# Second feed-forward block: four rounds of sevens instead of three, sums laid out anew

## The chip, the core and the metric

The kernel runs on one core of one Trainium2 chip. It is one launch that computes a whole decoder layer. The metric is the device time of that launch in microseconds, from its first to its last instruction and what lies around it. Three runs of the kernel before gave 854.62, 854.68 and 855.35 us; the median is 854.68 us. TensorE is PE in the profile, VectorE is DVE, ScalarE is ACT, GpSimd is POOL and SyncE is SP.

## The reference

The layer works on 512 tokens of width 1024 in f32, with an inner width of 22 x 128 = 2816:

```python
def swiglu(x, w_gate, w_up, w_down):
    return (jax.nn.silu(x @ w_gate) * (x @ w_up)) @ w_down

x = x + 0.5 * swiglu(rms_norm(x, g_ffn1[l]), w_ffn1_gate[l], w_ffn1_up[l], w_ffn1_down[l])
...          # attention in a window, convolution, attention to 256 memory tokens, and their output matrix
x = x + 0.5 * swiglu(rms_norm(x, g_ffn2[l]), w_ffn2_gate[l], w_ffn2_up[l], w_ffn2_down[l])
```

The change concerns the two feed-forward lines, and the second above all.

## The kernel before

Activations lie transposed: a tile has 128 features on the partitions and the 512 tokens along the row. Every f32 operand is cut in two parts, a rounded one ("hi", made by an ACT cast) and what is left of it ("lo", made by a DVE subtraction). One product then is three matmuls, hi x hi, hi x lo and lo x hi, which all add to one PSUM bank.

**The walk over f.** A block goes through 22 slices f of the inner width. For each slice it needs gate and up (the function `fast`, from f = 3 in the second block), and `hidden` then cuts the result, the tile u of slice f, in hi and lo. Gate and up come as seven products of 256 tokens each in place of eight, in Strassen's manner. For this `make_sums` builds four sums of the two raw weight tiles g and u on DVE (two go to s12, two to s43). Each of the seven products has 4 k-tiles x 3 = 12 matmuls, so a slice has 84.

**The rounds.** The down projection isn't kept for the end. The 22 slices are grouped in rounds, and while the slices of one round are computed, the products of the round before are put in between: one step, a quarter of a round, for every slice. In a plain round a step is `down`: for two output tiles it runs slices x 2 halves x 3 matmuls each, and DVE adds the result to x (L749). In a round "by sevens" (`inside`) four slices make two pairs, and a step is seven products of 2 x 3 = 6 matmuls, 42 in all. It needs its own sums: `four` builds four of the weights (L147 to L150), and `paired` builds four of the hidden slices once for each pair (L498 to L501) and cuts them (L478). ACT halves the results into four staging tiles (cosb, sinb, mk, mv; L516), and four DMAs that POOL issues add them to x (L547). The DMA with mk goes to the same tile of x as the one with cosb and is issued when that has landed; the one with mv likewise after sinb.

**The last round.** When slice 21 is computed, the steps that are left over ("post") run, and then `seven` for g = 0 to 3: four times 42 matmuls, whose order on PE, DVE and ACT is the order of the code. The first, g = 0, adds a part of its result to x0 and x1 through two DMAs of POOL (L567). Each `leave` (L575) reads PSUM and x on DVE and sends a tile to the output; the leaves of g run in the round g + 1, behind the weight work that is done ahead there.

**The order.** Outside the last round a scheduler of the framework sets each engine's order by its priorities, bound by the marks in the code (`issue_after`). The buffers are rings. Four raw weight tiles (wraw) are filled by SP's queue. Four cut weight tiles (w) are written by ACT and DVE as soon as PE is through with the one used four items earlier. Three "sum" tiles hold the sums.

## Time and profile before

| | before |
|---|---|
| median of three runs | 854.68 us |
| the profiled execution, its own time | 856.12 us |
| its span, first to last instruction | 854.0 us |
| PE busy | 844.8 us (99%), 6325 matmuls |
| DVE busy | 734.6 us (86%), 1288 instructions |
| ACT busy | 503.7 us (59%), 894 instructions |
| POOL busy | 77.4 us (9%), 86 instructions |
| granted TensorE clock, mean over the span | 0.998 |
| first matmul of the down products after slice 21 | 822.04 us |
| first matmul of `seven`, g = 0 | 830.20 us |
| last matmul starts | 849.24 us |

Times of the trace count from the start of the span. A row of the timeline gives start, length, engine, line and operation, and how many instructions it stands for; in square brackets stands how long the engine was idle before it and what ended that. Two instructions of an engine overlap a little, so the distance between two starts, not the length, says what an instruction costs its queue.

### The profile page before, as it was taken

To read this page: it belongs to the slowest core of one execution; us is meant where nothing else is said; L and a number is where in the kernel's file an instruction comes from. 1 tells how busy PE (TensorE), PEld (TensorE's weight loads), DVE (VectorE), ACT (ScalarE), POOL (GpSimd) and SP (SyncE) were. 2 spreads that over 40 slices of the span, in tenths; PEclk is the share of its full clock that TensorE was granted. 3 is DMA by queue.
4 is the path that set the end of the run, shared out by engine and by line. 5 is a ranking of instruction groups with operands and counts; after the bars stand their busy time and mean duration, and the time that the engine had idled before them with its cause. 6 is when DMAs were issued, how large, how long until landed. Compare 5 with 4: busy or idle time off the path is not lost. (4 is left out here: it accounts for less than half of the span.)

```text
span 854.0 us, 16045 instructions
## 1 busy us (share of the span) xinstructions
PE 844.8 (99%) x6325; PEld 782.2 (92%) x6325; DVE 734.6 (86%) x1288; ACT 503.7 (59%) x894; POOL 77.4 (9%) x86
## 2 busy tenths in 40 slices
PE   8999999999999999999999999999999999999997
PEld 5889999999999999988676788889999999999997
DVE  7998899697877897959988986799879988987897
ACT  7455567655564444632848764666545577767454
POOL 0000002210000000400000021220000022212000
PEclk9999999999999999999999999999999999999999
DMA  7435338764454334232001332873423378787524
GB/s 274 125 88 147 93 120 198 173 161 137 124 160 125 124 111 131 76 99 62 13 26 38 88 100 86 197 160 105 126 93 111 112 182 189 158 199 169 142 74 124
DMA packets 43419, 107.19 MB, mean 126 GB/s; under 512 B 4176, under 2 KB 8784, under 8 KB 43344
## 3 DMA queue, kind: packets, MB, share of 16 engines
q1 hardware_dynamic: 32032, 85.99, 32.3%
q0 software_dynamic: 10160, 18.62, 12.9%
q10 hardware_dynamic: 1152, 1.57, 0.6%
q8 instruction: 49, 0.80, 0.4%
q14 instruction: 26, 0.21, 0.1%
HBM read 88.07 MB, written 2.10 MB: 106 GB/s over the span
## 5 line engine op out<-in xcount | busy, mean ns | idle before, releaser
L675 PE MATMUL mm<-bh,w 128*128 128x256 f32 x888 | 245.7, 277 | 0.3 <-ACT kept L693 0.2
L676 PE MATMUL mm<-bl,w 128*128 128x256 f32 x888 | 245.3, 276 | 0.0
L677 PE MATMUL mm<-bh,w 128*128 128x256 f32 x888 | 245.3, 276 | 0.0
L675 PEld LDWEIGHTS mm<-bh,w 128*128 128x128 f32 x888 | 166.7, 188 | 0.8 <-ACT kept L693 0.7
L676 PEld LDWEIGHTS mm<-bl,w 128*128 128x128 f32 x888 | 166.7, 188 | 0.1
L677 PEld LDWEIGHTS mm<-bh,w 128*128 128x128 f32 x888 | 166.7, 188 | 0.0
L214 ACT CAST w<-wraw 128x1024 fp32r<-128x1024 f32 (+2 forms) x107 | 106.7, 1001 | 81.8 <-PE mm L421 35.7
L219 DVE TENSOR_TENSOR w<-wraw,w 128x1024 fp32r<-128x1024 f32 (+2 forms) x101 | 117.8, 1171 | 12.5 <-ACT w L214 11.4
L219 DVE TENSOR_TENSOR w<-s,w 128x1024 fp32r<-128x1024 f32 x90 | 109.8, 1220 | 17.9 <-ACT w L214 14.4
L214 ACT CAST w<-s 128x1024 fp32r<-128x1024 f32 x90 | 94.5, 1051 | 41.3 <-PE mm L677 24.9
L420 PE MATMUL mm<-hl,w 128*128 128x256 f32 (+1 forms) x392 | 114.5, 293 | 0.1
L421 PE MATMUL mm<-hh,w 128*128 128x256 f32 (+1 forms) x392 | 114.2, 292 | 0.0
L419 PE MATMUL mm<-hh,w 128*128 128x256 f32 (+1 forms) x392 | 114.0, 293 | 0.1
L420 PEld LDWEIGHTS mm<-hl,w 128*128 128x128 f32 x392 | 73.6, 188 | 2.8 <-DVE hl L634 0.7
L419 PEld LDWEIGHTS mm<-hh,w 128*128 128x128 f32 x392 | 73.4, 188 | 2.9 <-ACT hh L633 0.8
L421 PEld LDWEIGHTS mm<-hh,w 128*128 128x128 f32 x392 | 73.6, 188 | 2.1
L419 PE MATMUL mm<-xh,w 128*128 128x512 f32 x176 | 69.8, 401 | 0.6 <-ACT w L230 0.5
L420 PE MATMUL mm<-xl,w 128*128 128x512 f32 x176 | 69.3, 394 | 0.5 <-DVE xl L431 0.5
L421 PE MATMUL mm<-xh,w 128*128 128x512 f32 x176 | 69.0, 392 | 0.0
L704 ACT ACTIVATE t<-t 128x512 f32<-128x512 f32 x37 | 23.4, 633 | 52.1 <-DVE t L703 52.0
L160 DVE TENSOR_TENSOR s<-wraw 128x512 f32<-128x512 f32 x37 | 25.5, 689 | 32.2 <-DMA wraw<-in_wgu 31.9
L513 PE MATMUL mm<-h,w 128*128 128x256 f32 x180 | 49.8, 277 | 0.4 <-DVE w L219 0.4
(299 smaller groups left out, 1857.6 us busy)
## 6 DMA issues: line engine op xcount, KB each, us to landing
wraw<-in_wgu SPq DMA_DIRECT2D x86, 512.0 KB, 3.8
wraw<-in_wd SPq DMA_DIRECT2D x38, 512.0 KB, 3.7
wraw<-in_win SPq DMA_DIRECT2D x12, 512.0 KB, 3.5
x<-cosb POOLq DMA_DIRECT2D x12, 256.0 KB, 5.5
x<-sinb POOLq DMA_DIRECT2D x12, 256.0 KB, 5.3
x<-mk POOLq DMA_DIRECT2D x12, 256.0 KB, 4.4
x<-mv POOLq DMA_DIRECT2D x12, 256.0 KB, 5.4
wraw<-in_wd SPq DMA_DIRECT2D x8, 384.0 KB, 3.5
```

The lines of the kernel that those rows point to most:

```text
L160: nc.vector.tensor_tensor(s12[:, l], u[:, l], u[:, r], op=ALU.add)
L214: nc.scalar.copy(hi[:, :cols], raw[:, :cols])
L219: nc.vector.tensor_tensor(lo[:, :cols], raw[:, :cols], hi[:, :cols].bitcast(F32), op=ALU.subtract)
L419: PE.matmul(ps[:, t], wh[:, w], hi(k)[:, t], start=one, stop=False, skip_group_check=cut > 1)
L420: PE.matmul(ps[:, t], wh[:, w], lo(k)[:, t], start=False, stop=False, skip_group_check=cut > 1)
L421: PE.matmul(ps[:, t], wl[:, w], hi(k)[:, t], start=False, stop=end, skip_group_check=cut > 1)
L513: PE.matmul(ps, w[1][:, s], hi, start=False, stop=q == 1, skip_group_check=not first)
L675: PE.matmul(ps, wh[:, c], bh[k][:, block], start=one, stop=False, skip_group_check=not first)
L676: PE.matmul(ps, wh[:, c], bl[k][:, block], start=False, stop=False, skip_group_check=not first)
L677: PE.matmul(ps, wl[:, c], bh[k][:, block], start=False, stop=end, skip_group_check=not first)
L704: ACT.activation(g, g, AF.Silu)
```

## The change

In the second block the rounds are cut otherwise and one more goes by sevens: 0-2, 3-5, 6-9, 10-13, 14-17, 18-21, of which the last four are by sevens (before: 0-2, 3-6, 7-10, 11-14, 15-17, 18-21, with sevens in the third, fourth and last). The post steps of slice 21 become one `inside` step in place of two `down` steps.

The sums take less room in both blocks. The ring "sum" has two tiles in place of three. Of the four sums of gate and up, one stays in a tile of its own (s4), and one is written over the left half of the raw up tile; the two are therefore cut apart, as two pieces of 512 in place of one of 1024. The sums of a pair of hidden slices go to a tile m7 and, for the other two, over the tile of the even slice itself.

The pair 20/21 keeps its cut parts in the tiles bh and bl of the block's input. `hidden` is issued early at each start of a round, and otherwise in a slice with an `inside` step not before the last of the sums of `four` (`W.mark`). In the last round `ahead`, which casts the next weights and builds their sums, is called after the copy of the product T1 in place of first of all.

```diff
-SUM_BUFS = 3
+SUM_BUFS = 2
...
-        nc.vector.tensor_tensor(s3, a11, a21, op=ALU.subtract)
+        self.mark = nc.vector.tensor_tensor(s3, a11, a21, op=ALU.subtract).ins
...
-        s43 = self.extra.tile([P, 1024], F32, tag="sum", name=f"s43_{i}", bufs=SUM_BUFS)
+        s4 = self.extra.tile([P, 512], F32, tag="s4", name=f"s4_{i}", bufs=1)
         l, r = slice(0, 512), slice(512, 1024)
         nc.vector.tensor_tensor(s12[:, l], u[:, l], u[:, r], op=ALU.add)
+        nc.vector.tensor_tensor(u[:, l], g[:, l], u[:, l], op=ALU.add)
         nc.vector.tensor_tensor(s12[:, r], g[:, l], s12[:, l], op=ALU.add)
-        nc.vector.tensor_tensor(s43[:, l], g[:, r], s12[:, r], op=ALU.add)
-        nc.vector.tensor_tensor(s43[:, r], g[:, l], u[:, l], op=ALU.add)
-        self.sums[i] = (s12, s43)
+        nc.vector.tensor_tensor(s4, g[:, r], s12[:, r], op=ALU.add)
+        self.sums[i] = (s12, [(l, s4), (r, u[:, l])])
...
-    2: Plan([(0, 3), (3, 7), (7, 11), (11, 15), (15, 18), (18, 22)], 3, (2, 3, 5)),
+    2: Plan([(0, 3), (3, 6), (6, 10), (10, 14), (14, 18), (18, 22)], 3, (2, 3, 4, 5)),
...
-            m = pool.tile([P, 1024], F32, tag="sum", name=nm("h7"), bufs=SUM_BUFS)
-            t1, t2, t4, t3 = (m[:, c * 256 : c * 256 + 256] for c in range(4))
+            e, first = even[f - 1]
+            el, er = e[:, :256], e[:, 256:]
+            if ends:
+                hi, lo = (pool.tile([P, 7, 256], F32R, tag=tag, name=nm(tag), bufs=4) for tag in ("bh", "bl"))
+                split(hi[:, 0], lo[:, 0], el)
+            m = pool.tile([P, T], F32, tag="m7", name=nm("m7"), bufs=1)
+            t1, t2 = m[:, :256], m[:, 256:]
             DVE.tensor_tensor(t1, er, el, op=ALU.subtract)
             DVE.tensor_tensor(t2, r, t1, op=ALU.subtract)
-            DVE.tensor_tensor(t4, t2, l, op=ALU.subtract)
-            DVE.tensor_tensor(t3, r, er, op=ALU.subtract)
+            DVE.tensor_tensor(el, t2, l, op=ALU.subtract)
+            DVE.tensor_tensor(er, r, er, op=ALU.subtract)
...
-            W.split_to(W.at + 4)
-            if g < 2:
-                W.four(W.items[W.at + 4][0])
+            def ahead():
+                W.split_to(at + 4)
+                if g < 2:
+                    W.four(W.items[at + 4][0])
+
+            at = W.at
             wa, ws = W.next(), W.next()
...
             prod(de[:, r], ws, 0, 128, H_T1, True)
             half(s45[:, r], de[:, r])
+            ahead()
             while later:
                 leave(*later.pop(0))
...
-            if waiting and f - 1 in seven_at and seven_at.get(f) != seven_at[f - 1]:
+            if waiting and any(hi == f for _, hi in plan.rounds):
...
-            with tc.issue_after(mark.ins):
+            with tc.issue_after(mark.ins), tc.issue_after(W.mark) if seven else nullcontext():
...
             for d in post:
-                for step in down(*d):
+                for step in (inside if d[0] in plan.seven else down)(*d):
                     step()
```

PE has 6041 instructions in place of 6065 in the built program, DVE 1303 in place of 1239, ACT 906 in place of 833 and POOL 106 in place of 90.

DVE where a new round of sevens begins while the round before it was by sevens too, in the kernel before at slice 15. t_8256 is the tile of slice 14, h_804 takes the four sums of the pair 13/14, L478 makes lo parts of hidden slices, s_138 takes the sums that `four` builds, and w_8501 is the cut tile of those sums, which the `inside` step of this slice needs from its third product on:

```order
L500 TENSOR_TENSOR h_804_8472<-h_804_8472,t_8256 128x256
L501 TENSOR_TENSOR h_804_8472<-t_8256,t_8047 128x256
L478 TENSOR_TENSOR h_806_8478<-t_8256,h_805_8477 128x512
L148 TENSOR_TENSOR s_138_8502<-s_138_8502,wraw_8262 128x256
L478 TENSOR_TENSOR h_808_8482<-h_804_8472,h_807_8481 128x512
L478 TENSOR_TENSOR h_810_8486<-h_804_8472,h_809_8485 128x512
L149 TENSOR_TENSOR s_138_8502<-wraw_8262,s_138_8502 128x256
L150 TENSOR_TENSOR s_138_8502<-wraw_8262 128x256
L160 TENSOR_TENSOR s_139_8561<-wraw_8361 128x512
L163 TENSOR_TENSOR s_139_8562<-wraw_8350,wraw_8361 128x512
L219 TENSOR_TENSOR w_8501<-s_138_8502,w_8501 128x1024
```

The same engine in the changed kernel at slice 14, where its new round begins. L506 to L508 are the sums of the pair 12/13 and w_8387 is the cut tile of the sums of `four`:

```order
L506 TENSOR_TENSOR m_795_8358<-t_8140,m_795_8358 128x256
L508 TENSOR_TENSOR t_7929<-t_8140,t_7929 128x256
L507 TENSOR_TENSOR t_7929<-m_795_8358,t_8140 128x256
L478 TENSOR_TENSOR h_797_8364<-t_8140,h_796_8363 128x512
L219 TENSOR_TENSOR w_8387<-s_136_8388,w_8387 128x1024
L478 TENSOR_TENSOR h_799_8368<-m_795_8358,h_798_8367 128x512
L161 TENSOR_TENSOR wraw_8245<-wraw_8234,wraw_8245 128x512
L478 TENSOR_TENSOR h_801_8372<-t_7929,h_800_8371 128x512
```

The lo part of the sums now stands ahead of two of the three lo parts of the hidden slices, and `four` has been built earlier.

ACT in the last round, g = 1, before. L208 and L214 cast the weights of g = 2 (w_9885, then their sums w_9907), and L516 are the first two of the round's four copies, of the products 11 and T1:

```order
L208 CAST w_9885<-wraw_9669 128x512
L208 CAST w_9885<-wraw_9669 128x256
L214 CAST w_9907<-s_160_9844 128x1024
L516 ACTIVATE s_903_9905<-mm_9902 128x256
L516 ACTIVATE s_904_9906<-mm_9903 128x256
```

And in the changed kernel, where w_10030 and w_10072 are the weights of g = 2 and L528 are the same two copies:

```order
L208 CAST w_10030<-wraw_9807 128x512
L208 CAST w_10030<-wraw_9807 128x256
L528 ACTIVATE s_910_10050<-mm_10047 128x256
L528 ACTIVATE s_911_10051<-mm_10048 128x256
L214 CAST w_10072<-s_160_10009 128x1024
```

The cast of the sums went behind the two copies. On DVE the order in this round is as before: the lo part of the sums, the four sums for g = 3, the two leaves of g = 0, two additions to x, and the lo parts for g = 3. On POOL the two DMAs of g = 0 now stand right behind the four of the post step.

More of the change, by code (lines that the diff above doesn't have):

```diff
@@ L22 @@
 import math
-from contextlib import ExitStack
+from contextlib import ExitStack, nullcontext
 import numpy as np
@@ L328, in ffn_weights @@
             for d in post:
-                W.add(down(*d), OTHER if d[0] else WIDE)
+                (W.add_seven if d[0] in plan.seven else W.add)(down(*d), OTHER if d[0] else WIDE)
             if memory and f == MEM_F:
@@ L488, in paired @@
             n = seven_at[f]
+            ends = last and f >= NF - 2
             if not (f - plan.rounds[n][0]) % 2:
-                both = atile("h7")
-                first = both[:, :256], both[:, 256:]
-                split(*first, l)
-                even[f] = l, r, first
-                return
-            el, er, first = even[f - 1]
-            m = pool.tile([P, 1024], F32, tag="sum", name=nm("h7"), bufs=SUM_BUFS)
-            t1, t2, t4, t3 = (m[:, c * 256 : c * 256 + 256] for c in range(4))
+                first = None
+                if not ends:
+                    both = atile("h7")
+                    first = both[:, :256], both[:, 256:]
+                    split(*first, l)
+                even[f] = t, first
+                return
+            e, first = even[f - 1]
[5 more added lines that the diff above has]
+            t1, t2 = m[:, :256], m[:, 256:]
             DVE.tensor_tensor(t1, er, el, op=ALU.subtract)
             DVE.tensor_tensor(t2, r, t1, op=ALU.subtract)
-            DVE.tensor_tensor(t4, t2, l, op=ALU.subtract)
-            DVE.tensor_tensor(t3, r, er, op=ALU.subtract)
-            h_l, h_r = two(t)
-            h_t1, h_t2 = two(m[:, :512])
-            h_t4, h_t3 = two(m[:, 512:])
+            DVE.tensor_tensor(el, t2, l, op=ALU.subtract)
+            DVE.tensor_tensor(er, r, er, op=ALU.subtract)
+            if ends:
+                for c, part in ((1, t), (3, m), (5, e)):
+                    split(hi[:, c : c + 2], lo[:, c : c + 2], part.rearrange("p (a m) -> p a m", a=2))
+                first, h_l, h_r, h_t1, h_t2, h_t4, h_t3 = ((hi[:, c], lo[:, c]) for c in range(7))
+            else:
+                h_l, h_r = two(t)
+                h_t1, h_t2 = two(m)
+                h_t4, h_t3 = two(e)
             sevens[n].append([first, h_l, h_t1, h_t2, h_t4, h_t3, h_r])
@@ L681, in fast @@
             l, r = slice(0, 256), slice(256, 512)
+            seven = any(d[0] in plan.seven for d in mid)
             b, de, c = mm_bank()[:, l], mm_bank(), sc_bank()[:, l]
@@ L709, in fast @@
                 rest.pop(0)()
-            seven = any(d[0] in plan.seven for d in mid)
             if seven:
```

## The prediction

> **What bounds the kernel now.** I read the page first, then the stretches of the second block, the waits of PE, and last the timeline of DVE, ACT and POOL over the final 25 us. The page gives busy time, share of the span and instructions:
>
> ```profile
> PE 844.8 (99%) x6325; PEld 782.2 (92%) x6325; DVE 734.6 (86%) x1288; ACT 503.7 (59%) x894; POOL 77.4 (9%) x86
> ```
>
> PE is the bound over the span, so a matmul taken away ought to count in full. The stretches say where this holds. Columns: from:to, length, busy us and instructions of PE, PEld, DVE, ACT and POOL, clock, DMA share, GB/s. The first two lie in the steps by sevens, 822.04 to 830.20 in the two `down` steps after slice 21, and the last four are the rounds g = 0 to 3:
>
> ```profile
> 712.00:726.00 14.00, 14.00 (x126) 14.00 (x125) 11.71 (x18) 9.92 (x19) 3.31 (x4) 1.00 0.86 208
> 726.00:740.00 14.00, 13.58 (x119) 13.38 (x118) 13.96 (x26) 10.20 (x19) 3.42 (x4) 1.00 0.74 151
> ...
> 822.04:830.20 8.16, 8.16 (x74) 8.16 (x73) 7.50 (x15) 4.44 (x8) 0.00 (x0) 1.00 0.07 27
> 830.20:834.96 4.76, 4.76 (x44) 4.76 (x43) 4.39 (x9) 3.26 (x7) 1.16 (x2) 1.00 0.00 0
> 834.96:839.72 4.76, 4.76 (x44) 4.76 (x43) 3.62 (x8) 3.30 (x8) 0.58 (x1) 1.00 0.66 114
> 839.72:844.48 4.76, 4.76 (x44) 4.76 (x43) 4.76 (x8) 2.52 (x6) 0.00 (x0) 1.00 0.30 112
> 844.48:849.30 4.82, 4.82 (x44) 4.82 (x42) 4.64 (x9) 1.54 (x4) 0.00 (x0) 1.00 0.50 186
> ```
>
> A round has 42 matmuls and takes 4.76 us, so a matmul of 256 tokens costs PE 0.1133 us. PE loses time in only one of these stretches, and there DVE is full. In the rounds g = 2 and 3 DVE is full too. Its timeline there:
>
> ```profile
> 836.29 1.23 DVE L219 TENSOR_TENSOR w<-s,w 128x1024 fp32r<-128x1024 f32 x1 [0.53 <-ACT w L214]
> 837.43 0.42 DVE L147 TENSOR_TENSOR s<-wraw 128x256 f32<-128x256 f32 x1
> ...
> 838.69 0.42 DVE L150 TENSOR_TENSOR s<-wraw 128x256 f32<-128x256 f32 x1
> 839.64 1.29 DVE L575 SCALAR_TENSOR_TENSOR t<-mm,x 128x512 f32<-128x512 f32 x2 [0.54 <-DMA x<-s]
> 840.85 1.28 DVE L565 TENSOR_TENSOR x<-x,s 128x512 f32<-128x512 f32 x2
> 842.05 1.02 DVE L209 TENSOR_TENSOR w<-wraw,w 128x512 fp32r<-128x512 f32 x2
> 842.99 1.22 DVE L219 TENSOR_TENSOR w<-s,w 128x1024 fp32r<-128x1024 f32 x1
> 844.12 1.28 DVE L575 SCALAR_TENSOR_TENSOR t<-mm,x 128x512 f32<-128x512 f32 x2
> 845.32 1.28 DVE L565 TENSOR_TENSOR x<-x,s 128x512 f32<-128x512 f32 x2
> 846.69 1.29 DVE L575 SCALAR_TENSOR_TENSOR t<-tp,x 128x512 f32<-128x512 f32 x2
> 847.90 0.68 DVE L565 TENSOR_TENSOR x<-x,t 128x512 f32<-128x512 f32 x1
> 848.50 0.69 DVE L565 TENSOR_TENSOR x<-x,kept 128x512 f32<-128x512 f32 x1
> 849.27 1.35 DVE L575 SCALAR_TENSOR_TENSOR t<-mm,x 128x256 f32<-128x256 f32 x3
> ```
>
> From 839.64 to 850.62 (849.27 + 1.35) no row shows a wait: 10.98 us of DVE work in one piece, and the leave that opens it waits 0.54 us for the DMA that adds to x1. So the end of the kernel is not set by PE alone. It is the start of that first leave plus 10.98 us, plus 3.4 us of output to the span's 854.0. Counted from the start of g = 0 at 830.20, the leave starts at +9.44.
>
> **The change, part by part.** The sum is made for the profiled execution: 856.12 us, 2.1 more than its span and 1.44 more than the median of the runs.
>
> *Matmuls.* The round 3-5 has three slices in place of four: its 8 output tiles lose 6 matmuls each, 48. The round 14-17 replaces a plain round of three slices, 8 x 18 = 144, by four steps of 42 = 168. Together -24, times 0.1133: **-2.72 us**, all before g = 0, where PE is full.
>
> *The stall at 736.* A row of PE, the one before it, and the DVE rows that lead there:
>
> ```profile
> 730.94 0.68 DVE L478 TENSOR_TENSOR h<-t,h 128x512 fp32r<-128x512 f32 x1
> ...
> 735.01 1.23 DVE L219 TENSOR_TENSOR w<-s,w 128x1024 fp32r<-128x1024 f32 x1
> ```
> ```profile
> 735.60 0.28 PE L512 MATMUL mm<-h,w 128*128 128x256 f32 x1
> 736.29 0.39 PE L513 MATMUL mm<-h,w 128*128 128x256 f32 x1 [0.42 <-DVE w L219]
> ```
>
> From 735.60 to 736.29 are 0.69 us where 0.11 are due: 0.58 lost, because the lo part of the sums stands behind the pair's work and seven further instructions. In the new order it stands right behind the first lo part, and only two rows behind L506 to L508: in the rows above the sequence from 730.94 to 735.01 shrinks from 4.07 us to one instruction of 0.60. There are now two such starts (14 and 18). I take **-0.58** for the old one and nothing for the two new ones; at worst each costs what the old one did, +1.16.
>
> *DVE and ACT in the steps.* 37 cuts of one 1024-wide tile become two of 512. By distance of starts 1024 cost 1.13 (842.99 to 844.12) and two of 512 cost 1.20 (840.85 to 842.05): +0.07 a slice. A new step by sevens brings four sums (1.67, 837.43 to 839.10) and cuts of 512 and 256 (0.94, 842.05 to 842.99), and drops two additions to x (1.20), so +1.4 us in a slice. The steps then look as from 712 to 740, where DVE was busy 25.67 of 28 us and PE lost only the stall above: cost 0, bounded above by that +1.16. The in-place sums wait for nothing new: what they overwrite was read just before on the same engine. The ring of two holds one s12 and one set of `four`, where three held s43 too.
>
> *After slice 21.* PE's cover falls from 72 matmuls (8.16 us) to 42 (4.76 us). Behind it the hidden parts of the pair must be ready:
>
> ```profile
> 823.73 0.69 DVE L722 TENSOR_TENSOR t<-t,t 128x512 f32<-128x512 f32 x1
> ...
> 828.88 0.68 DVE L478 TENSOR_TENSOR h<-h,h 128x512 fp32r<-128x512 f32 x1
> ```
>
> From the end of slice 21's product (823.73 + 0.69) to the last of these parts were 5.14 us, but with four additions to x (2.4 us) among them that are gone. What is left is one cut of sums (1.13), three sums (1.25) and three cuts (1.8), 4.2 us: ready 2.4 + 4.2 = 6.6 after 822.04, or earlier. The first of the three is wanted at 4.76 + 6 x 0.1133 + 0.34 = +5.8 and is ready 1.2 before the last, at +5.4. Nothing is lost; 1 us at the upper bound.
>
> *The casts behind the copies.* This is the part that costs. ACT in the round g = 1, which begins on PE at 834.96:
>
> ```profile
> 835.21 1.05 ACT L214 CAST w<-s 128x1024 fp32r<-128x1024 f32 x1 [0.20 <-ACT w L208]
> ...
> 837.20 0.38 ACT L516 ACTIVATE s<-mm 128x256 f32<-128x256 f32 x1 [0.66 <-PE mm L513]
> ...
> 838.56 0.38 ACT L516 ACTIVATE s<-sc 128x256 f32<-128x256 f32 x1 [0.30 <-PE sc L513]
> 838.84 0.92 ACT L208 CAST w<-wraw 128x512 fp32r<-128x512 f32 x2
> ```
>
> The copy of T1 starts 2.24 into the round and can't be earlier, since PE must have done 18 matmuls. The cast now stands behind it: 0.28 later (838.56 to 838.84), at +2.52. Its lo part follows 1.08 after the cast's start (835.21 to 836.29): +3.60. Then 1.14 for it, 1.67 for the four sums (837.43 to 839.10, where the wait of the leave begins), and the leave can start at +6.41, where it started at +4.68 (839.64 - 834.96). Behind it queue, on DVE, the additions, the weights of g = 3 and all that follows, the whole 10.98 us. **+1.73 us**, if the DMA doesn't wait longer than that.
>
> *The POOL queue.* The two DMAs to x0 and x1 used to find POOL empty. Now the post step's four stand ahead of them, and the fourth (mv) waits until the second (sinb) has landed. Such pairs before, the two DMAs of g = 0, and the time to landing of these two:
>
> ```profile
> 742.99 0.86 POOL L547 DMA_DIRECT2D x<-sinb  x1 [0.81 <-ACT sinb L516]
> 746.84 0.86 POOL L547 DMA_DIRECT2D x<-mv  x1 [0.86 <-ACT w L214]
> ...
> 757.28 0.86 POOL L547 DMA_DIRECT2D x<-sinb  x1 [0.83 <-ACT sinb L516]
> 763.77 0.87 POOL L547 DMA_DIRECT2D x<-mv  x1 [1.09 <-ACT w L214]
> ...
> 833.80 1.74 POOL L567 DMA_DIRECT2D x<-s  x2 [42.62 <-DVE s L148]
> ```
> ```profile
> DMA to landing us min/median/max: 4.5/4.8/5.1
> ```
>
> sinb to mv took 3.85 us where no weights were being loaded and 6.49 where they were; after slice 21 all weights but the last are there, so I take 3.9. An estimate from the parts above: the last hidden cast of ACT ends at about -0.1, a weight cast of 0.92 follows, and the copy to sinb behind them ends at about +0.9 (-0.7 without them); its DMA is issued at +1.1. Then mv at +5.0, x0 at +5.9, x1 at +6.6, and x1 landed 5.1 later at +11.7. The leave is ready at 4.76 + 6.41 = +11.2 by the part above, so the DMA ends last: the leave starts at +11.7 where it was +9.44, **+2.26 us** in place of 1.73. Bounds: +1.73 (DMA early) and, with 6.49 for sinb, +4.9.
>
> [...]
>
> Sum: -2.72 - 0.58 + 2.26 = **-1.04 us**. 856.12 becomes 855.1 in the profile, and the median 854.68 becomes 853.6.
>
> **The rivals.**
> (A) *The end gives back less.* If x1 lands early, the leave costs 1.73 and the time is 854.68 - 2.72 - 0.58 + 1.73 = 853.1; if the end has room that the rows don't show, nothing is given back and it is 851.4. For it: DVE still waited at 836.29 (0.53), so its piece isn't full all the way back, and a DMA that meets no weight loads may land faster than 5.1. Against it: from 839.64 on the rows follow each other without a wait.
> (B) *Slower: the POOL queue decides.* It sits at the mv DMA ahead of x0 and x1. From +12.7 on for x1's landing (a loss of 3.3) the change gains nothing. With 6.49 us for sinb and 6.5 for x1, since mv, x0 and x1 then fly together: 1.1 + 6.49 + 0.9 + 0.7 + 6.5 = +15.7, a loss of 6.3, and 854.68 - 3.30 + 6.3 = 857.7. For it: 6.49 was seen. Against it: only where weights were loading.
> (C) *DVE is the bound of the steps.* Four more slices with steps and pairs, at 25.67 of 28 us: two stalls like 736's and 1 us after slice 21 make 853.6 + 2.2 = 855.8, no difference that can be told.
>
> **How the numbers follow.** Within 0.2% (1.7 us, about what a measurement of this kernel can tell from no change) means 852.97 to 856.39. My forecast of 853.6, with its own range 852.6 to 855.0, has 0.45. A has 0.33, of which 0.28 lies below 852.97; B 0.13; C 0.09. Faster: 0.28 from A and 0.06 from the forecast's lower edge, 0.34. Slower: B, 0.13. Same: the rest of the forecast and of A, and C, 0.53. The range 851.4 to 855.9 leaves out B's far end and what lies below A.
>
> **What would show it.** 24 matmuls fewer (6301) and the first matmul of g = 0 about 3.3 us earlier confirm the gain; no stall of PE on a cut of sums at a round's start confirms the order. The first leave (two of 512 on DVE behind four sums) should start 11 to 12 us after that matmul, wait for the DMA to x, and be followed by 11 us of DVE without a gap; PE should wait about 1.1 us in g = 3 for the cut sums (11.7 + 4.57 by the rows above, where 14.28 + 0.91 is wanted). If the leave starts at +9.5, or the end follows it by less than 14 us, the end's part is wrong and A holds. If x1's landing is beyond +12.7, B. If PE waits for weights between slices 6 and 21, C.

## The result: slower by 0.56%, and the profile after

The changed kernel takes 860.29 us (median of 6 runs, 857.54 to 861.87), the kernel before beside it 854.65 (6 runs): a ratio of 1.0056, 95% interval 1.0041 to 1.0070. On a second chip it was 1.0042 (1.0028 to 1.0055). The forecast was 853.6, no change.

The page's busy line of the changed kernel:

```profile
PE 842.1 (98%) x6301; PEld 779.3 (91%) x6301; DVE 744.3 (87%) x1353; ACT 518.3 (61%) x967; POOL 91.0 (11%) x102
```

PE has the 24 matmuls less, 2.7 us of work. It has new waits, in the list of waits by engine (engine, line, what it waited for: us in total, times, longest):

```profile
PE mm L691 <- ACT kept L710: 2.9, 2, 1.7
...
PE mm L525 <- DVE w L219: 0.5, 1, 0.5
PE mm L523 <- ACT s L528: 0.5, 1, 0.5
```

L691 is the first matmul of a product of gate and up, L710 the copy of the product Q1 on ACT; before, this wait had 0.2 us. To see where the time goes I use the first copy of a slice (L686 before, L703 now) as a milestone: in six of the eight rows below it starts 0.31 to 0.32 us after the start of the twelfth matmul of the slice's first product, and in the changed kernel's rows at slices 3 and 11, where ACT is still at a cast, 0.57 and 0.75. The kernel before, ACT's timeline at slices 4 and 21 of block 1 and 3 and 11 of block 2:

```profile
71.64 0.37 ACT L686 COPY kept<-mm 128x256 f32<-128x256 f32 x1 [0.28 <-PE mm L677]
...
321.92 0.37 ACT L686 COPY kept<-mm 128x256 f32<-128x256 f32 x1 [0.27 <-PE mm L677]
...
573.48 0.37 ACT L686 COPY kept<-mm 128x256 f32<-128x256 f32 x1 [0.28 <-PE mm L677]
...
671.76 0.37 ACT L686 COPY kept<-mm 128x256 f32<-128x256 f32 x1 [0.39 <-PE mm L677]
```

The changed kernel at the same four places:

```profile
71.09 0.37 ACT L703 COPY kept<-mm 128x256 f32<-128x256 f32 x1 [0.28 <-PE mm L693]
...
323.26 0.37 ACT L703 COPY kept<-mm 128x256 f32<-128x256 f32 x1 [0.27 <-PE mm L693]
...
573.46 0.36 ACT L703 COPY kept<-mm 128x256 f32<-128x256 f32 x1
...
672.34 0.39 ACT L703 COPY kept<-mm 128x256 f32<-128x256 f32 x1
```

And its last rounds, in the table of stretches (the post step from 823.43, then g = 0 to 2):

```profile
823.43:828.79 5.36, 5.21 (x45) 4.97 (x43) 4.40 (x9) 4.43 (x10) 0.86 (x1) 1.00 0.09 20
828.79:834.35 5.56, 5.07 (x45) 4.87 (x43) 4.01 (x8) 5.30 (x13) 1.71 (x2) 1.00 0.74 126
834.35:839.11 4.76, 4.76 (x45) 4.76 (x43) 3.22 (x7) 2.94 (x8) 2.62 (x3) 1.00 0.85 144
839.11:843.87 4.76, 4.76 (x45) 4.76 (x43) 4.31 (x10) 2.43 (x6) 0.00 (x0) 1.00 0.50 135
```

Stage by stage (us; "due" is the difference in matmuls times 0.1133):

| stretch | before | after | difference | due |
|---|---|---|---|---|
| start to slice 4, block 1 | 71.64 | 71.09 | -0.55 | 0 |
| slices 4 to 21, block 1 | 250.28 | 252.17 | **+1.89** | 0 |
| on to slice 3, block 2 | 251.56 | 250.20 | -1.36 | 0 |
| slices 3 to 11, block 2 | 98.28 | 98.88 | +0.60 | -0.68 |
| on to the first post matmul | 150.28 | 151.09 | +0.81 | +1.36 |
| post to g = 0 | 8.16 | 5.36 | -2.80 | -3.40 |
| g = 0 to the first leave | 9.44 | 12.35 | **+2.91** | 0 |
| leave to the end of the span | 14.36 | 14.36 | 0 | 0 |
| sum | 854.0 | 855.5 | +1.5 | -2.72 |

By that twelfth matmul instead of the copy, the three rows that meet at slices 3 and 11 read -1.62, +0.41 and +1.25 in place of -1.36, +0.60 and +0.81. And one row must be read with care. The granted clock from 450 to 460 us, first the kernel before and then the changed one (the third column from the right):

```profile
450.00:460.00 10.00, 10.00 (x78) 7.84 (x78) 8.89 (x55) 9.03 (x28) 0.00 (x0) 0.83 0.14 45
```
```profile
450.00:460.00 10.00, 9.78 (x86) 7.73 (x84) 9.70 (x55) 10.00 (x33) 0.00 (x0) 1.00 0.23 76
```

The profiled execution of the kernel before had a dip of the clock there that the changed one didn't have. Eight of the 17 profiles here have it, and the stretch that holds it, from slice 21 of block 1 to slice 3 of block 2, takes 251.4 to 252.0 us in them and 250.0 to 251.1 in the others, so it accounts for most of the -1.36. The first row can't be put down to the change either: up to slice 4 the 17 profiles take 70.8 to 72.1 us, and two profiles of the changed kernel 71.09 and 71.74. Without these two rows the profiles differ by 1.5 + 1.36 + 0.55 = 3.4 us, and that is what the second chip measured (858.85 against 855.44). Five of the six timed runs of the first measurement had a mean clock of 0.996 to 0.998; on the second chip the three runs of the changed kernel at 0.996 took 860.8 to 861.0 us, so the clock is a likely part of the first measurement's 5.6.

**Where PE waits.** Slice 16 of block 1, in the changed kernel: DVE, ACT and PE.

```profile
229.73 0.69 DVE L160 TENSOR_TENSOR s<-wraw 128x512 f32<-128x512 f32 x1 [3.95 <-DMA wraw<-in_wgu]
...
235.69 0.68 DVE L738 TENSOR_TENSOR t<-t,t 128x512 f32<-128x512 f32 x1
```
```profile
236.40 0.62 ACT L649 CAST hh<-t 128x512 fp32r<-128x512 f32 x1 [3.63 <-DVE t L738]
...
237.87 0.38 ACT L710 ACTIVATE kept<-mm 128x256 f32<-128x256 f32 x1
```
```profile
236.29 0.28 PE L693 MATMUL mm<-bh,w 128*128 128x256 f32 x1
238.30 0.39 PE L691 MATMUL mm<-bh,w 128*128 128x256 f32 x1 [1.73 <-ACT kept L710]
```

Read it backwards. PE waits for the copy of Q1. The copy stands on ACT behind the cast of slice 15's hidden tile. That cast waits for DVE's product (L738), and DVE stood still for 3.95 us until a raw up tile had landed (that of slice 17: DVE's sums run a slice ahead). In the kernel before, ACT at the same slice has the other order, the copy of Q1 (L693) ahead of the hidden cast (L633):

```profile
233.22 0.37 ACT L686 COPY kept<-mm 128x256 f32<-128x256 f32 x1 [0.27 <-PE mm L677]
...
236.00 0.38 ACT L693 ACTIVATE kept<-mm 128x256 f32<-128x256 f32 x1 [0.32 <-PE mm L677]
236.28 0.62 ACT L633 CAST hh<-t 128x512 fp32r<-128x512 f32 x1
```

The change issues `hidden` early at each start of a round, and slice 16 of block 1 is one. So two things meet in this stall, the early cast and the late load. Slice 5 of block 2 has another form of it. DVE and ACT there:

```profile
592.92 0.69 DVE L161 TENSOR_TENSOR wraw<-wraw,wraw 128x512 f32<-128x512 f32 x1
593.52 0.69 DVE L738 TENSOR_TENSOR t<-t,t 128x512 f32<-128x512 f32 x1
594.13 1.22 DVE L219 TENSOR_TENSOR w<-wraw,w 128x1024 fp32r<-128x1024 f32 x1
595.26 0.69 DVE L162 TENSOR_TENSOR s<-wraw,s 128x512 f32<-128x512 f32 x1
```
```profile
596.06 1.05 ACT L214 CAST w<-s 128x1024 fp32r<-128x1024 f32 x1 [3.31 <-DVE s L162]
597.01 0.38 ACT L710 ACTIVATE kept<-mm 128x256 f32<-128x256 f32 x1
```

No load is late here. The sum in place (L161) has taken the slot of s2 (L162); s2 follows 2.34 us later behind two other instructions, its cast follows it, and the copy of Q1 stands behind the cast. PE waits 1.15 us for that copy.

**Why the load is late.** The loads between 213 and 226 us, SP's queue of the kernel before and then of the changed one:

```profile
215.19 0.38 SPq L178 DMA_DIRECT2D wraw<-in_wd  x1
219.86 2.43 SPq L178 DMA_DIRECT2D wraw<-in_wgu  x2
```
```profile
219.74 0.38 SPq L178 DMA_DIRECT2D wraw<-in_wd  x1
222.67 1.47 SPq L178 DMA_DIRECT2D wraw<-in_wgu  x2
```

The first of these loads, of a down tile, takes the buffer of the raw up tile of slice 15. DVE before, the first sum of the up tile of slice 16 and then the last reader of that of slice 15:

```profile
210.92 0.69 DVE L160 TENSOR_TENSOR s<-wraw 128x512 f32<-128x512 f32 x1 [1.12 <-DMA wraw<-in_wgu]
...
214.47 0.69 DVE L219 TENSOR_TENSOR vlo<-wraw,vhi 128x512 fp32r<-128x512 f32 x1
```

and in the changed kernel, where the last reader is the cut of the sum that lies in the tile:

```profile
213.67 0.69 DVE L160 TENSOR_TENSOR s<-wraw 128x512 f32<-128x512 f32 x1 [4.43 <-DMA wraw<-in_wgu]
...
219.02 0.69 DVE L209 TENSOR_TENSOR w<-wraw,w 128x512 fp32r<-128x512 f32 x1
```

215.16 against 219.71 is when the reader ends, and the load is issued 0.03 us later, 6.07 us after the first sum shown, where it was 4.27 before. But nothing waits for this down tile here. What DVE waits for is the pair of gate and up behind it, and in both kernels that pair is issued about 9.0 us after the first sum shown (219.86 - 210.92 and 222.67 - 213.67), 0.03 us after DVE has cut an older raw tile (at 219.83 and 222.64). So the pair is late because that sum is, and the sum is late because it waited 4.43 us for the up tile of slice 16 in place of 1.12. That tile's load was issued at 207.28 us, before at 207.04. From there to its landing, the kernel before and then the changed one:

```profile
DMA to landing us min/median/max: 3.8/3.8/3.8
```
```profile
DMA to landing us min/median/max: 6.4/6.4/6.4
```

It is a loop here: the load that landed later made DVE's first sum 2.75 us later, and with it the next pair 2.81. The down tile and the pair stood closer together in the changed kernel (issued at 203.20, 206.14 and 207.28 against 200.62, 204.81 and 207.04), since the raw up tile held the first of them. Whether that slowed the landing no run here tests.

### The profile page after: what moved, and what is told of

Read it like the earlier page. It is cut to its first block, busy times and chain, and to the rows that moved or that the text cites. A ratio compares the mean times of both kernels' runs of the same rounds, so it can differ in the third digit from the quotient of the medians.

```text
span 855.5 us, 16165 instructions
## 1 busy us (share of the span) xinstructions
PE 842.1 (98%) x6301; PEld 779.3 (91%) x6301; DVE 744.3 (87%) x1353; ACT 518.3 (61%) x967; POOL 91.0 (11%) x102
## 5 line engine op out<-in xcount | busy, mean ns | idle before, releaser
L691 PE MATMUL mm<-bh,w 128*128 128x256 f32 x888 | 246.0, 277 | 2.9 <-ACT kept L710 2.9
L693 PE MATMUL mm<-bh,w 128*128 128x256 f32 x888 | 245.2, 276 | 0.0
L691 PEld LDWEIGHTS mm<-bh,w 128*128 128x128 f32 x888 | 166.7, 188 | 3.7 <-ACT kept L710 3.5
L693 PEld LDWEIGHTS mm<-bh,w 128*128 128x128 f32 x888 | 166.7, 188 | 0.0
L214 ACT CAST w<-wraw 128x1024 fp32r<-128x1024 f32 (+2 forms) x103 | 102.4, 999 | 72.2 <-issue 32.7
L219 DVE TENSOR_TENSOR w<-wraw,w 128x1024 fp32r<-128x1024 f32 (+2 forms) x97 | 113.0, 1168 | 10.8 <-ACT w L214 10.7
L421 PE MATMUL mm<-hh,w 128*128 128x256 f32 (+1 forms) x328 | 96.9, 296 | 0.1
L420 PE MATMUL mm<-hl,w 128*128 128x256 f32 (+1 forms) x328 | 96.9, 296 | 0.0
L419 PE MATMUL mm<-hh,w 128*128 128x256 f32 (+1 forms) x328 | 96.3, 296 | 0.0
L219 DVE TENSOR_TENSOR w<-s,w 128x1024 fp32r<-128x1024 f32 x57 | 69.6, 1221 | 21.4 <-ACT w L214 19.2
L214 ACT CAST w<-s 128x1024 fp32r<-128x1024 f32 x57 | 59.8, 1049 | 16.0 <-ACT kept L703 6.5
L420 PEld LDWEIGHTS mm<-hl,w 128*128 128x128 f32 x328 | 61.6, 188 | 2.5 <-DVE hl L650 0.4
L421 PEld LDWEIGHTS mm<-hh,w 128*128 128x128 f32 x328 | 61.6, 188 | 2.5 <-DVE w L219 0.3
L419 PEld LDWEIGHTS mm<-hh,w 128*128 128x128 f32 x328 | 61.4, 188 | 2.5 <-ACT hh L649 0.4
L523 PE MATMUL mm<-h,w 128*128 128x256 f32 x210 | 58.7, 279 | 0.8 <-ACT s L528 0.5
L525 PE MATMUL mm<-h,w 128*128 128x256 f32 x210 | 58.2, 277 | 0.5 <-DVE w L219 0.5
L524 PE MATMUL mm<-h,w 128*128 128x256 f32 x210 | 58.0, 276 | 0.0
```

Source lines behind the costliest of these rows:

```text
L214: nc.scalar.copy(hi[:, :cols], raw[:, :cols])
L219: nc.vector.tensor_tensor(lo[:, :cols], raw[:, :cols], hi[:, :cols].bitcast(F32), op=ALU.subtract)
L419: PE.matmul(ps[:, t], wh[:, w], hi(k)[:, t], start=one, stop=False, skip_group_check=cut > 1)
L420: PE.matmul(ps[:, t], wh[:, w], lo(k)[:, t], start=False, stop=False, skip_group_check=cut > 1)
L421: PE.matmul(ps[:, t], wl[:, w], hi(k)[:, t], start=False, stop=end, skip_group_check=cut > 1)
L523: PE.matmul(ps, w[0][:, s], hi, start=first and q == 0, stop=False, skip_group_check=not first)
```

## The experiments

Ratios are to the kernel before, run beside it on the same chip; the chip is not the same in all experiments. Two things for the quoted expectations: they count the slices of block 1 from slice 4, so "slice 12" there is slice 16; and each was written before its run, the first with a theory that did not survive it.

### The raw tile, the order of the sums

```diff
-        s4 = ...[P, 512]...                        # s3_apart: g + u in a tile of its own,
-        nc.vector.tensor_tensor(u[:, l], g[:, l], u[:, l], op=ALU.add)
+        s43 = ...[P, 1024]..., bufs=1
+        nc.vector.tensor_tensor(s43[:, r], g[:, l], u[:, l], op=ALU.add)
-            m = pool.tile([P, T], F32, tag="m7", ...)
+            m = kept()
```

> The changed kernel, but the sum g + u of gate and up gets half a tile of its own again, in place of the left half of the raw up tile; the 2 KB for it come from m7, whose sums go to the ring kept. Still cut in two pieces of 512, same plan, same last round. Theory (the sum in place holds the raw up tile until its cut, 4 us longer, so the next three weight loads are issued some 3 us later, and a load that lands late stalls DVE, then ACT, then PE): the loads of gate and up near 220 us are issued about 3 us earlier, the two stalls of PE on the copy of Q1 (1.73 and 1.15 us) are gone, the runs lie within 1.5 us of each other, and the median falls from 860.3 to between 855 and 857. Rival 1 (the extra round by sevens brings 16 more adding DMAs, which slow the loads): the median stays above 859. Rival 2 (POOL's queue ahead of the last round scatters): the stalls go, but the median stays above 858.5.

Measured 1.0046 (1.0028 to 1.0063), 859.09 us. The expected 855 to 857 did not come. Both stalls shrink, to 0.53 and 0.79 us, but in the steps by sevens two new ones of 0.5 appear at the same copy. The raw tile comes free early again, the down tile's load is issued at 218.01, 3.65 us after the first sum (214.36). And yet the pair of gate and up was no earlier (223.35), again 9.0 us after that sum. So the raw tile alone is not the cause. With one buffer for s43 the sum g + u has to stand behind the cut of the slice before; that this is what takes its place is not shown.

```diff
-        nc.vector.tensor_tensor(s43[:, r], g[:, l], u[:, l], op=ALU.add)   # before_inplace,
-        self.sums[i] = (s12, s43)                                          # from the kernel before
+        nc.vector.tensor_tensor(u[:, l], g[:, l], u[:, l], op=ALU.add)
+        self.sums[i] = (s12, [(l, s43[:, l]), (r, u[:, l])])
```

> The kernel before with one edit: the sum g + u is written over the left half of the raw up tile and is cut from there, in two pieces of 512. Plan, ring of three and last round as before. Theory of the raw tile: the loads come later here too, PE stalls on copies in both blocks, and the time rises by 2 to 5 us, to 856.7 to 859.7, with more scatter than the 1.4 us of the kernel before. Rival 1 (the extra round's DMAs) and rival 2 (POOL's queue at the end): within 0.7 us of 854.65, since neither is in this kernel.

Measured 1.0011 (0.9999 to 1.0023), 856.31 against 855.55: not told from no change, and below what the theory wanted. In its profile slice 16 takes 16.34 us where 14.96 are due (132 matmuls), the loss of 1.4 that the theory names; nothing else of that size moves. `hidden` is in its old place here, and PE does not wait for the copy of Q1: its longest waits in that slice are for lo parts of DVE, 0.22 and 0.56 us. So the early cast decides which wait shows the loss, and isn't needed for it.

> The changed kernel itself, for a second profile on the chip of the next three. The first profile of it had a granted clock of 1.00 from 450 to 460 us, where that of the kernel before had 0.83, which cost it 1.25 us in the stretch 369 to 469. So the difference between the two kernels at an equal clock is about 2.75 us in the profiles, and the runs add what the clock takes. Theory: the stalls near 236 and 596 us come back at the same places with 1.5 to 2 and 1.0 to 1.4 us, since they follow from the order and from when the raw tile is released; the median lies 4 to 6 us above the kernel before. Rival (loads that land late by chance): the stalls are at other places or gone.

Measured 1.0042 (1.0028 to 1.0055). The median is 3.4 us above the kernel before, under the 4 to 6 expected. The stalls come back at the same copies with 1.73 and 0.91 us, and one of 0.96 more earlier in slice 16, where PE waits for DVE's addition to x. The load of gate and up that slice 16 waits for took 231.20 - 221.93 = 9.3 us from its issue to the sum, where the first profile had 229.73 - 222.67 = 7.1.

```diff
+        nc.vector.tensor_tensor(s12[:, r], g[:, l], s12[:, l], op=ALU.add)  # sum_order: s2 first,
         nc.vector.tensor_tensor(u[:, l], g[:, l], u[:, l], op=ALU.add)      # then the sum in place
-        nc.vector.tensor_tensor(s12[:, r], g[:, l], s12[:, l], op=ALU.add)
```

> The changed kernel with two lines of make_sums exchanged: the sum s2 (the right half of s12) is made ahead of the sum that goes over the raw up tile, as it was before the change. Theory (the sum in place stands ahead of s2 on DVE, s12 is ready later, its cast stands ahead of the copy of Q1 on ACT, and PE waits for that copy): the stall near 596 us falls from 1.2 to under 0.4, the one near 236 by 0.6; 858 to 859 if the changed kernel is at 860.3. Rival (ring of two: s12 waits for a buffer): no change.

Measured 1.0023 (1.0008 to 1.0038), 857.89, which is 1.0 less than the changed kernel beside it. Both stalls are gone. ACT at the place shown above, in this kernel:

```profile
593.48 1.05 ACT L214 CAST w<-s 128x1024 fp32r<-128x1024 f32 x1 [0.98 <-PE mm L693]
594.86 0.39 ACT L710 ACTIVATE kept<-mm 128x256 f32<-128x256 f32 x1 [0.33 <-PE mm L693]
```

The cast now waits for PE, not for DVE, and is 2.6 us earlier. In block 1 the gain was partly luck: the load landed early here (228.18), and the stall near 236 returned in two later kernels with the same lines (best2, best3). In the last round the leave came 13.59 us after g = 0, later than in the changed kernel (12.35), which hides a part of the gain.

```diff
-    (all of make_sums as changed; m7)                     # sums_old
+    (make_sums as before, s43 with one buffer, cut whole; m = kept())
```

> The changed kernel with make_sums word for word as it was: s43 in a tile of 1024 of its own (one buffer), cut whole, g + u last; m7 in the ring kept to make room. Plan and last round as changed. Theory (the raw tile and the order of the sums are the two causes in front of the last steps): both stalls are gone, and 1.5 to 3.2 us are won: 857 to 858.8 if the changed kernel is at 860.3. Rival (the extra round's DMAs and DVE work): 859.5 or more.

Measured 1.0016 (0.9999 to 1.0032), 857.56. That is 1.3 us below the changed kernel beside it (858.85), where the theory wanted 1.5 to 3.2. Stalls of 0.45 to 0.7 us remain in slices 12 and 16 of block 1 and of 0.5 at two copies in block 2: one buffer is not the ring of three.

```diff
+        nc.vector.tensor_tensor(s43[:, r], g[:, l], u[:, l], op=ALU.add)   # before_order, from the
         nc.vector.tensor_tensor(s12[:, r], g[:, l], s12[:, l], op=ALU.add) # kernel before
         nc.vector.tensor_tensor(s43[:, l], g[:, r], s12[:, r], op=ALU.add)
-        nc.vector.tensor_tensor(s43[:, r], g[:, l], u[:, l], op=ALU.add)
```

> The kernel before with the lines of make_sums in the order of the change (g + u ahead of s2), each sum still in its own tile; nothing else. Theory (only the order of these two sums makes s12 late, its cast on ACT late, and the copy of Q1 behind it): PE stalls on that copy here too, near 236 and near 587 or 596 us, 1 to 1.9 us each, and the time rises by 1.5 to 3 us. Rival (the stalls need the later loads or the ring of two as well): within 0.7 us of the kernel before.

Measured 0.9987 (0.9978 to 0.9996): not slower. The theory that the order by itself makes the stall fell: slice 16 of block 1 loses nothing here, and slice 5 of block 2 takes 9.87 us in place of 9.52. The order costs its price only together with the new layout.

### Block 1

What the profiles have in common is the lead of DVE over PE in block 1: from the start of the first sum (L160) ahead of slice 16, which follows the landing of the up tile of slice 17, to the first copy of slice 16. Beside it, what slice 16 took over its 14.96 us:

| layout of the sums in block 1 | kernels | lead, us | loss in slice 16, us |
|---|---|---|---|
| as before | before, before_order, best4, b1_order, b1_old | 5.9, 5.3, 5.7, 5.7, 4.2 | 0, 0, 0, 0, 0.2 |
| in place, ring of three | before_inplace | 3.2 | 1.4 |
| own tile, one buffer | s3_apart, best1, sums_old | 3.4, 2.7, 2.6 | 0.8, 1.2, 1.4 |
| in place, s2 first | sum_order, best2, best3 | 4.4, 2.7, 2.5 | 0.4, 2.1, 2.4 |
| as changed | end_both, after, pool_order, ahead_first, after_again | 2.8, 2.7, 2.5, 1.9, 1.6 | 2.0, 2.2, 2.3, 2.9, 3.2 |

The new layout takes 1.5 to 4.3 us of lead, whichever half of it is undone. With 5.3 us and more nothing is lost, with 4.4 and less 0.2 to 3.2, and how much it is depends on when the load lands: in the five kernels as changed, lead and loss add up to 4.8 or 4.9 us each time. What in the layout takes the lead stays open.

```diff
+        (self.make_sums_2 if self.last else self.make_sums_1)(i)      # b1_old: block 1 with make_sums,
-                paired(f, t)                                          # paired, ring of three and the
+                (paired if last else paired_1)(f, t)                  # condition for hidden of before
```

> The changed kernel with block 1 alone in its old layout, all of block 2 as changed. Theory: the stall near 236 (1.7 to 2.7 us) goes, the one near 596 (0.9 to 1.2) and the late first leave stay: 3.0 to 3.6 us above the kernel before, where the changed kernel is 3.4 to 5.6 above it. Rival (block 1 isn't where it is lost): no change against the changed kernel.

Measured 1.0022 (1.0012 to 1.0032), 856.95 against 855.06: 1.9 us above the kernel before, less than the 3.0 to 3.6 expected. No stall near 236; the one in slice 5 of block 2 stays with 0.75, and the leave is late, 13.23 us after g = 0. Block 1 was worth 0.2 to 0.34%. The edit brings back the layout and the old place of `hidden` together; the share of each was not measured.

```diff
     (b1_old, and the two lines of sum_order exchanged)    # b1_order
```

> The changed kernel with block 1 in its old layout and, in block 2, s2 made ahead of the sum in place; the last round as changed. It differs from the run with the old block 1 alone by the exchange of two lines in block 2. Theory: the stall near 596 (0.75 us there) is gone and 0.8 to 1.3 us are won in block 2, of which the wait of the first leave for the DMA to x1 may take some back, since that DMA hangs on POOL's queue and not on PE: a ratio of 1.0007 to 1.0015, where the old block 1 alone had 1.0022. Rival (the exchange helped by chance, through the load in block 1): the same ratio as the old block 1 alone, and the stall is still there.

Measured 0.9997 (0.9980 to 1.0014), below the 1.0007 to 1.0015 expected. Slice 5 of block 2 takes 9.52 us, exactly its 84 matmuls, where it took 10.58 in b1_old. Within the new layout the order has its price by itself: about 0.25% between these two, on different chips and with intervals that touch, of which the profile shows 1.1 us in this slice.

### The last round

The leave that opens the end, in the changed kernel, and POOL's DMAs ahead of it:

```profile
841.14 1.29 DVE L587 SCALAR_TENSOR_TENSOR t<-mm,x 128x512 f32<-128x512 f32 x2 [0.38 <-DMA x<-s]
```
```profile
830.48 0.86 POOL L559 DMA_DIRECT2D x<-sinb  x1 [1.84 <-ACT sinb L528]
831.55 0.86 POOL L559 DMA_DIRECT2D x<-mk  x1 [0.22 <-ACT s L528]
834.37 0.86 POOL L559 DMA_DIRECT2D x<-mv  x1 [1.96 <-ACT w L208]
834.91 2.09 POOL L579 DMA_DIRECT2D x<-s  x2
```

```diff
-                for to, part in ((x0, s12), (x1, s45), (x0, o0), (x1, o1)):   # pool_order: of the post
+                for to, part in ((x0, s12), (x1, s45)):                       # step, mk and mv are held
...
-                add(x1, s45)
+                mark = add(x1, s45)
+                if g == 0:
+                    with tc.issue_after(mark):
+                        held.pop()()
```

> The changed kernel, but of the last step's four DMAs the two with mk and mv are issued behind the two DMAs of g = 0 to x0 and x1. All else as changed. By the trace of the changed kernel the first leave waits 0.38 us for the DMA to x1, so by the theory of the raw tile this is worth 0.3 to 0.5 us: 859.8 to 860. Rival 2 (POOL's queue is what makes the timed runs slower and uneven): 857 to 858, with the runs within 1.5 us.

Measured 1.0032 (1.0022 to 1.0043), 858.48. In the profile the leave no longer waits for a DMA and starts 11.89 us after g = 0, 0.46 earlier, as the theory had it. The median lies between the two forecasts, and its interval overlaps that of the changed kernel on either chip; it does not tell them apart.

```diff
-            ahead()                                 # ahead_first: behind the copy of T1
+            ahead()                                 # and now first in each round
```

> The changed kernel with the casts and sums for the next rounds again first of all in each round of the last four, not behind the copy of T1. By the prediction's step this alone is worth 1.73 us where DVE decides, but the leave then waits for the DMA to x1, which is not earlier: it starts at +11.55 less 0.38 at the earliest by DVE, +11.5 by the DMA. Theory: 859.9 to 860.3, no gain that can be told. If the casts behind the copies and not the DMA set the end: 858.3 to 858.7.

Measured 1.0044 (1.0029 to 1.0059), no gain. DVE is through with its sums early, and then:

```profile
842.88 0.69 DVE L587 SCALAR_TENSOR_TENSOR t<-mm,x 128x512 f32<-128x512 f32 x1 [1.52 <-DMA x<-s]
```

The wait for the DMA grows from 0.38 to 1.52 us. In g = 0 the early cast stands ahead of the copies on ACT and stops PE for 1.47.

```diff
     (pool_order, and ahead() first where g > 0, behind the copy where g == 0)   # end_both
```

> The changed kernel with the two corrections of the last round alone: the DMAs to x0 and x1 ahead of those of mk and mv, and the casts first again in g = 1 and 2. Theory: the first leave comes 1.6 to 2.1 us earlier against the end of slice 21 and all of it reaches the end: 1.5 to 2 us less than the changed kernel. The sum of the two causes ahead of it is then what is left above the kernel before, 2 to 3 us.

Measured 1.0018 (1.0007 to 1.0029), 857.48. That is 2.4 us above the kernel before, within the 2 to 3 expected. The leave starts 10.62 us after g = 0, 1.73 earlier than in the changed kernel. Each of the two corrections alone gave 0.46 us or nothing; together they give 1.73 of the 2.91 lost there, since either the cast or the DMA was enough to hold the leave.

### Together

> As the run with the old make_sums, and in the last round the two DMAs to x0 and x1 go ahead of those of mk and mv, and the casts for the next rounds come first of all again in g = 1 and 2 (in g = 0 behind the copies, where the cast first of all made PE wait 1.47 us). Theory (DVE behind the cast, and the DMA behind mv, set the first leave together): the leave starts about +9.5 to +10 after the first matmul of g = 0, and 1.6 to 2.1 us come back against the run with the old make_sums alone; with it the time should be 0 to 1.5 us above or below the kernel before. Rival (the end is set elsewhere): no gain over the run with the old make_sums.

This is sums_old with end_both. Measured 1.0001 (0.9985 to 1.0018), 855.86 against 855.44, as expected, though the leave at +10.67 is later than the 9.5 to 10 of the theory.

> The changed kernel with s2 made ahead of the sum in place, the DMAs to x0 and x1 ahead of those of mk and mv, and the casts first again in g = 1 and 2. Theory: -2.72 for the matmuls, -0.6 for the stall at 736, +1.0 after slice 21, and the leave about as early after g = 0 as before: 1.8 to 2.6 us below the kernel before, a ratio of 0.9970 to 0.9980. Rival (the two corrections overlap, or the loads that come later still cost): a ratio of 0.999 to 1.001, as the run with the old make_sums had.

sum_order with end_both. Measured 0.9989 (0.9980 to 0.9998), 855.57 against 856.24. Less than expected. Its profile has the stall near 236 again:

```profile
236.88 0.28 PE L709 MATMUL mm<-bh,w 128*128 128x256 f32 x1
238.85 0.39 PE L707 MATMUL mm<-bh,w 128*128 128x256 f32 x1 [1.69 <-ACT kept L726]
```

So the order of the sums does not cure block 1. This led to the table of leads above.

> As the run before it in this list, and in g = 0 the sums of four for g = 2 are built ahead of the cut of the weights of g = 1, in the 1.5 us in which DVE waits there for the cast. Theory: DVE is 0.5 to 1.5 us earlier at the first leave, unless the DMA to x1 ends later than that; 0 to 1 us less than without. Rival: the sums then stand in the way of slice 21's own work on DVE, and PE reaches g = 0 later by up to 1.7 us.

```diff
             def ahead():                               # best3: best2, and
+                if g == 0:
+                    W.four(W.items[at + 4][0])
                 W.split_to(at + 4)
-                if g < 2:
+                if g == 1:
                     W.four(W.items[at + 4][0])
```

Measured 0.9992 (0.9982 to 1.0002): the leave at +10.60 in place of +10.63. No gain; the early sums are not what holds it.

> s2 ahead of the sum in place, the DMAs to x0 and x1 first and the casts first in g = 1 and 2, as before, and block 1 gets its old layout back: ring of three, s43 and the sums of a pair in it, hidden as before. Only block 2 keeps the new layout. Theory (the layout takes away the lead that DVE has over PE in block 1, 5.9 us before slice 12 in the kernel before and 1.6 to 4.4 us in the changed kernels, and a load that lands late then stops PE): the lead is 5 us or more again, no stall of PE near 236, and 1.5 to 2 us less than with the new layout in block 1: a ratio of 0.9965 to 0.9975. Rival (the lead is lost to the state of the DMA queues and would be so in any kernel): a ratio of 0.9985 to 0.9995 as without.

best2 with block 1 as in b1_old. Measured **0.9966 (0.9953 to 0.9979)**, 852.49 against 855.06: as expected, faster than the kernel before, and by more than any version here. Its loads near 220 and its leave:

```profile
215.48 0.38 SPq L193 DMA_DIRECT2D wraw<-in_wd  x1
220.15 2.58 SPq L193 DMA_DIRECT2D wraw<-in_wgu  x2
```
```profile
836.69 0.68 DVE L634 SCALAR_TENSOR_TENSOR t<-mm,x 128x512 f32<-128x512 f32 x1
```

The loads are back at their old distance, 4.67 us. With the mean of the two measurements of the changed kernel, 1.0049, the three corrections taken singly give -0.26% (sum_order), -0.27% (b1_old) and -0.31% (end_both): their sum leads to 0.9965. Within intervals of 0.1 to 0.15% each they add up to the whole. What is left, 2.6 us, is close to the 24 matmuls alone (2.72). The leave of best4 still comes 10.56 us after g = 0, where it was 9.44.

## Why the prediction was wrong

- **The matmuls, -2.72.** Right in itself: 6301, and best4 shows that the time follows once the three causes are taken away (-2.6 us by its medians).
- **The stall at 736, -0.58.** Right in that the profile has no stall on a cut of sums at a round's start. What that gave is less sure: from slice 11 to the post step it has +0.81 by the copies and +1.25 by the twelfth matmul, where +1.36 is due.
- **"DVE and ACT in the steps", cost 0.** Wrong, and this step decides. Its sentences were "The in-place sums wait for nothing new: what they overwrite was read just before on the same engine" and that the ring of two holds what three did. They ask what the sum waits for, and not who waits for its tile: SP's load does, and it comes 4.55 us later in the place shown. The step was also costed from 712 to 740 us alone; the new layout and the early `hidden` hold for block 1 too, and slices without a step by sevens were never looked at. In block 1 it cost 1.89 us: the lead fell from 5.9 to 2.7 us, and it came back, to 4.2 to 5.7 us, where block 1 got its old form (b1_old, b1_order, best4). Which part of the new form takes the lead stays open, since undoing the sum in place (s3_apart), the order (sum_order, best2) or both (sums_old) did not bring it back. The order of the two sums cost 1.28 more in block 2 (0.60 where -0.68 was due; 1.09 by the twelfth matmul); with it exchanged the same eight slices take 97.58 us, the 97.60 that are due. The bound of 1.16 covered another mechanism.
- **After slice 21, 0 with a bound of 1.** 0.60: the post step took 5.36 us in place of 4.76. DVE was costed there, ACT wasn't: its four copies stand between the casts of the pair and of the weights. The same queue cost g = 0 another 0.80 (5.56 in place of 4.76), PE's wait for s.
- **The end, +2.26.** The mechanism was right, the size short: +2.91. The mv DMA stood 3.89 us behind sinb (3.9 taken), the DMA to x1 was issued 6.6 us after g = 0 as forecast, and landed 5.7 later where 5.1 was taken; that is the 0.65. The leave waited for it, and 10.98 us of DVE and 3.4 of output followed. The wait of 0.80 in g = 0 shows on DVE, which was ready for the leave at +12.0 in place of +11.2, still ahead of the DMA. The first matmul of g = 0 came 1.41 us earlier in place of 3.3, and in g = 3 PE waited 0.50 us for the cut sums in place of 1.1. The rows of 4.5 to 5.1 us to landing were the right ones to go by: the two DMAs here took 4.3 and 5.7, and in ahead_first the leave waits 1.52 for them. That sinb to mv takes 3.85 us without weight loads and 6.49 with them is not shown: within the 3.85 SP issued a down tile at 744.78 and gate and up from 745.68, and the DMA share was 0.92, against 0.97 within the 6.49.
- **The rivals.** B's 857.7 is the nearest to the time, but for another reason: x1 landed at +12.35, short of the +12.7 that B asks for, and POOL's queue was worth 0.46 us by itself. The 6.5 us that B takes for x1 were its estimate; x1 took 5.7. C named the right kind of place, two stalls in the slices, and found them too small and in the wrong block. None named the lead of the loads.

The sum of what was missed: 1.89 + 1.28 + 0.60 + 0.65 = 4.4 us on -1.04, which is 3.4 slower, the difference of the two profiles by the copies, without the dip of the clock and the start.

## What to carry to other kernels

When a result is written over an input, ask who refills the input's buffer and how much later it now comes free (4.55 us in the place shown). The lead that DVE lost here, 1.5 to 4.3 us, showed up two engines further on, as lost time of PE that varied from 0.4 to 3.2 us in slice 16. Count such a change in every stage that uses the same code. And where two queues held the same instruction, undoing one of them moved it by 0.46 us or not at all, and undoing both by 1.73: undo both before calling either harmless.

## What the hardware showed unasked

In eight of the 17 profiles, whichever kernel ran, the granted TensorE clock was at half for a time between 453 and 461 us, within the attention; in the others it stayed at 1.00. The mean over the span was 0.996 to 0.998 in the eight and 0.999 or 1.000 in the others. The kernel before, in stretches of 1 us:

```profile
453.00:454.00 1.00, 1.00 (x8) 0.71 (x7) 1.00 (x5) 1.00 (x4) 0.00 (x0) 0.93 0.00 0
454.00:455.00 1.00, 1.00 (x6) 0.67 (x6) 0.86 (x7) 1.00 (x5) 0.00 (x0) 0.50 0.15 41
...
457.00:458.00 1.00, 1.00 (x10) 0.83 (x9) 1.00 (x7) 0.69 (x3) 0.00 (x0) 0.87 0.00 0
```

0.07, three times 0.50 and 0.13 of a microsecond are missing from 453 to 458, 1.70 in all, and the stretch that holds them is about 1.1 us longer in the mean, as much as a term of the prediction. In stretches of 0.1 us the clock of the kernel before stands at 0.50 from 453.9 to 457.2, at 0.75 and 0.69 in the stretch ahead of that and the one behind it, and at 1.00 around them. best1 lacks 0.30, 0.50, 0.50 and 0.40 us from 454 to 458, 1.70 again. Why only some executions have the dip, no run here tests.

The same two loads of gate and up, 512 KB each, took 6.3 us (s3_apart, 223.35 to 229.68), 7.1 (the changed kernel) and 9.3 (after_again) from their issue to the sum that waits for them. The kernel before needed 7.5 (219.86 to 227.31) and lost nothing with its lead of 5.9 us; the other three, with 3.4, 2.7 and 1.6, lost 0.8, 2.2 and 3.2.
